# A hybrid attention trunk on one core: spare buffers for the last grouped head, work moved between VectorE and GpSimd, and a last tile in two parts

## The chip, the cores and the metric

One NeuronCore of a Trainium2 chip runs the whole program. The metric is device microseconds of one execution. A core has TensorE (PE in the profile, with its weight loads as PEld), VectorE (DVE), ScalarE (ACT), GpSimd (POOL) and SyncE (SP, which here issues nearly all DMAs). Each engine works through its own queue in order; semaphores order the queues among each other.

## The reference, cut to what matters

Two layers of a trunk with two token mixers side by side. There are 512 latent tokens and 256 context tokens, 1024 channels, and heads of 64. All data are float32.

```
hx = rmsnorm(x) * (1 + scale) + shift;  p = hx @ w_in        # all projections in one
a_att = neighbourhood attention of 8 heads (latent queries: window and all context keys)
b_att = grouped-query attention of 8 query heads over 2 key heads (all 768 keys)
o_a = (a_att * silu(a_z)) @ w_o_a ;  o_b = (b_att * silu(b_z)) @ w_o_b
merged = sigmoid(g_a) * o_a + sigmoid(g_b) * o_b
x = x + gate * (merged @ w_out)
```

Layer 0 does the same for the context tokens (they attend to the context alone); layer 1 needs only the latent ones, and what it gives is the output.

## The kernel before, in words

**High and low parts.** A float32 product is made of three TensorE products: each operand is split into a high part (a cast on ScalarE to a shorter float32) and a low part (the difference, on VectorE or GpSimd), and `mm3` (lines 351 to 353) adds high x high, high x low and low x high. A matrix of weights goes through a `raw` tile (three buffers, loaded by SP), then `whi` and `wlo` (a ring of eight each, in the pool `wp`). `load_w` and `load_w2` do this; their last argument picks the engine of the low part: `mix_lo` alternates GpSimd and VectorE, `pool_lo` takes GpSimd.

**Order.** The kernel is written in Python, and a planner turns it into the five queues: an instruction that stands earlier in the text has priority, later ones go ahead where the planner's model of time finds an engine free. Buffers come from rings: a tag has so many buffers, they are given out in the order of the text, and a tile waits until one is free.

**The stage around the change.** `pipeline` runs 8 grouped heads: `gq_scores(h)`, then `gq_values(h - 1)`, then a share of `fill` (pieces of the gates' and `w_o_a`'s projections, one bank `psf`). Behind the last scores come the rest of `fill`, then `early` (it splits quarters 0 to 2 of `zb` into `gbh` and `gbl` with `hilo`: cast on ScalarE, line 557; low part on GpSimd, line 558), and last `values_of(7)`.

`gq_values` handles six blocks of 128 keys. For each, `transpose_split` transposes the probabilities of the four query tiles with four TensorE products into a bank `pst` (line 669; two banks, tag `t`), ScalarE casts them to `pth` (line 672), VectorE forms `ptl` (line 673), both from rings of two, and TensorE adds two products into the bank `psv` (lines 972 and 973; one bank). In layer 0 a seventh block, `ctx_values`, follows for the context queries. `head_out` then copies one half of `psv` to `ho` (one buffer; line 681, ScalarE), adds the other half (line 682, VectorE) and multiplies the sum into `zb`, which holds the gate (line 683, GpSimd).

**The merge.** The banks of scores (`pss`, two of two banks each) and `psv` close, and five banks `psx` open. The last quarter of `zb` is split, and `o_chunks("b", ...)` multiplies it by `w_o_b`: four chunks of two `w_o_b` tiles, each chunk two column groups of four steps. `evac_b` merges into `tg` and splits the result into `mh` and `ml`. Then for each half `n` of `w_out` (eight tiles of 512 columns) and each tile `t` of 128 tokens, `tok_proj` runs 24 products, and `evac_o` multiplies by the gate (line 1039), adds `x` (line 1041) and, in layer 1, stores (line 1043).

Of the kernel before, what the change touches and what calls it, by code (L numbers as in the profile page):

```python
# [8 lines left out]
F32 = mybir.dt.float32  # L9
F32R = mybir.dt.float32r  # L10
BF16 = mybir.dt.bfloat16
AF = mybir.ActivationFunctionType
ALU = mybir.AluOpType
# [9 lines left out]
KT = DM // 128  # L23
# [35 lines left out]
def R(ap):  # L59
    return ap.bitcast(F32R)  # L60
# [7 lines left out]
def hybrid_kernel(es: ExitStack, tc, x, ctx, cvec, w_ada, w_ada0, small, gvec, w_in, w_o_a, w_o_b, w_out,  # L68
# [13 lines left out]
    def nm(s):  # L82
        uid[0] += 1
        return f"{s}_{uid[0]}"
# [26 lines left out]
    def psw(n=512, kind="w"):  # L111
        if kind == "w":
            kind = "f" if pm["i"] % pm["n"] == 0 else "x"
            pm["i"] += 1
        pool, cols = pm[kind]
        return pool.tile([128, cols], F32, tag=kind, name=nm("ps" + kind))[:, :n]
# [211 lines left out]
    def load_w2(src, col0, nk, lo_eng):  # L328

        res = []  # L330
        for i in range(nk // 2):
            raw = raw_tile()
            nc.sync.dma_start(raw.rearrange("p (k n) -> p k n", k=2),
                              src[256 * i:256 * i + 256, col0:col0 + 256].rearrange("(k p) n -> p k n", k=2))
            hi = wp.tile([128, 512], F32R, tag="whi", name=nm("whi"), bufs=8)
            S.copy(hi, raw)  # L336
            lo = wp.tile([128, 512], F32R, tag="wlo", name=nm("wlo"), bufs=8)
            lo_eng(i).tensor_tensor(lo, raw, F(hi), ALU.subtract)  # L338
            res += [(hi[:, c:c + 256], lo[:, c:c + 256]) for c in (0, 256)]
        return res  # L340
# [149 lines left out]
    def layer(l, hx, nxt, mid):  # L490
# [60 lines left out]
        def hilo_tiles(name):  # L551
            return [big(name + part).rearrange("p (f n) -> p f n", f=4) for part in "hl"]

        def hilo(src, dst, fs):
            sv = src.rearrange("p (f n) -> p f n", f=4)
            for f in fs:
                S.copy(R(dst[0][:, f, :ntok]), sv[:, f, :ntok])
                G.tensor_tensor(R(dst[1][:, f, :ntok]), sv[:, f, :ntok], dst[0][:, f, :ntok], ALU.subtract)

        def load_tg(c):  # L560
            nc.sync.dma_start(tg[c].rearrange("p (f n) -> p f n", f=4)[:, :, :ntok], gs[c][:, :, :ntok])
# [1 line left out]
        def o_chunks(br, prepare, evac):  # L563

            src = (w_o_a if br == "a" else w_o_b)[l]
            act = lambda part, k: gated[br][part][:, k, :]
            res = []
            for i in range(4):
                st = {}

                def ld(i=i, st=st):
                    st["w"] = load_w2(src, 256 * i, 4, mix_lo)
                pieces = [lambda f=f, n0=n0, n1=n1, i=i, st=st:
                          chan_proj(st["w"], f, act, n0, n1, lambda f, a, b, ps: evac(2 * i + f, a, b, ps))
                          for f in range(2) for n0, n1 in spans]
                res.append((ld, ([prepare] if i == 0 and prepare else []) + pieces))
            return res
# [72 lines left out]
        if True:  # L650
# [10 lines left out]

            def transpose_split(blocks, n0=0, n1=512):

                pt = psw(512, "t")
                for src, c0 in blocks:
                    if c0 is None:
                        T.transpose(pt.rearrange("p (s n) -> p s n", n=64)[:, 0:8:7, :], src, ident)
                    else:
                        T.transpose(pt[:, c0:c0 + 128], src, ident)  # L669
                hi = att["p"].tile([128, 512], F32R, tag="pth", name=nm("pth"), bufs=att["nt"])  # L670
                lo = att["p"].tile([128, 512], F32R, tag="ptl", name=nm("ptl"), bufs=att["nt"])
                S.copy(hi[:, n0:n1], pt[:, n0:n1])  # L672
                V.tensor_tensor(lo[:, n0:n1], pt[:, n0:n1], F(hi[:, n0:n1]), ALU.subtract)  # L673
                return hi, lo

            def head_out(po, e, dst):

                n = dst.shape[-1]
                m, o = 64 * e, 64 * (1 - e)
                t1 = att["p"].tile([128, 512], F32, tag="ho", name=nm("ho"), bufs=1)  # L680
                S.copy(t1[m:m + 64, :n], po[o:o + 64, :n])
                V.tensor_tensor(t1[m:m + 64, :n], po[m:m + 64, :n], t1[m:m + 64, :n], ALU.add)
                G.tensor_tensor(dst, dst, t1[m:m + 64, :n], ALU.mult)

            def rows(a, half):
                return a[64 * half:64 * half + 64]
# [69 lines left out]
            def open_att(name, width, n_p, n_t):  # L756
                st = ExitStack()
                att["p"] = st.enter_context(tc.tile_pool(name=name, bufs=2, reuse_waits="tile"))
                att["w"], att["np"], att["nt"] = width, n_p, n_t
                return st  # L760


# [74 lines left out]
            def pipeline(fill, spread, scores_of, values_of, last=None, bg=[]):  # L837

                n = len(fill)
                prev = None  # L840
                for h in range(8):
                    att["bg"] = bg if h > 3 or pm["n"] == 1 else []
                    st = scores_of(h)
                    if prev is not None:
                        values_of(h - 1, prev)
                    run(fill, len(fill) - (n - n * min(h + 1, spread) // spread))
                    prev = st
                if last is not None:
                    run(fill, len(fill))
                    last()  # L850
                run(bg, len(bg))
                values_of(7, prev)
                run(fill, len(fill))

# [140 lines left out]
        with tc.tile_pool(name=f"mrg{l}", bufs=1, reuse_waits="tile") as mp:  # L995
            open_ps(x=5)
            extra = lambda name: mp.tile([128, 3072], F32, tag="extra", name=nm(name))
            gv = mp.tile([128, nv, DM], F32, tag="gate", name=nm("gate"), bufs=1)
            for v in range(nv):
                src = gd[l][8 * v:8 * v + 8].rearrange("k p -> (k p)").unsqueeze(0)  # L1000
                nc.sync.dma_start(gv[:, v, :], src.to_broadcast([128, DM]))
            hilo(zb, gated["b"], [3])
            mg = []

            def evac_b(f, n0, n1, ps):
                a, b = tg_part(0, f, n0, n1), tg_part(1, f, n0, n1)
                V.scalar_tensor_tensor(b, b, 1.0, ps, ALU.add, ALU.mult)
                V.tensor_tensor(a, a, b, ALU.add)
                hi, lo = [m[:, f % 4, n0:n1] for m in mg[f // 4]]
                S.copy(R(hi), a)  # L1010
                V.tensor_tensor(R(lo), a, hi, ALU.subtract)
            chunks = o_chunks("b", None, evac_b)
            chunks[0][0]()
            for i in range(4):
                if i < 3:
                    chunks[i + 1][0]()
                if i % 2 == 0:
                    mg.append(hilo_tiles("m"))
                for piece in chunks[i][1]:
                    piece()  # L1020

            nt = 6 if first else 4
            xv = [a.rearrange("p (t n) -> p t n", t=3) for a in (big("xt0"), extra("xt1"))]
            xts = []
            for t in range(nt):
                xt = xv[t // 3][:, t % 3, :]
                nc.sync.dma_start(xt, x_src(t) if first else xs1[128 * t:128 * t + 128, :])
                xts.append(xt)
            a_m = lambda part, k: mg[k // 4][part][:, k % 4, :]
            bg = ada_steps(1, range(16), (1,), 2, mp) + [lambda: ada_mod(1)] if first else []  # L1030
            run(bg, 1)
            per_bg = -(-len(bg) // nt)
            for n in range(2):
                w = load_w(w_out[l], 512 * n, 512, KT, mix_lo)

                def evac_o(t, ps, n=n):
                    cs = slice(512 * n, 512 * n + 512)
                    t1 = mp.tile([128, 512], F32, tag="t1", name=nm("t1"), bufs=2)
                    V.tensor_tensor(t1, ps, gv[:, 0 if t < 4 else 1, cs], ALU.mult)
                    xt = xts[t]  # L1040
                    V.tensor_tensor(xt[:, cs], xt[:, cs], t1, ALU.add)
                    if not first:
                        nc.sync.dma_start(o_lat[16 * t:16 * t + 16][:, :, cs], xt[:, cs])
                    elif n == 1:
                        if t < 4:
                            nc.sync.dma_start(xs1[128 * t:128 * t + 128, :], xt)
                        late.append(lambda: make_hx(1, t, xt, nxt(), mp))
                late = []
                for t in range(nt):
                    tok_proj(w, 512, a_m, t, evac_o)  # L1050
                    run(bg, per_bg)
                    run(late, len(late) - 1)
                run(late, len(late))
# [186 lines left out]
```

## Time and profile before

| what | value |
|---|---|
| median of 3 runs | 1148.6 us (1148.3 to 1148.79) |
| the profiled execution, in full | 1149.07 us |
| its span in the profile | 1147.0 us |
| TensorE busy | 1123.5 us, 98% of the span |
| VectorE, ScalarE, GpSimd busy | 818.3, 580.3, 483.0 us |
| granted TensorE clock, mean | 0.999 |

A row of the timeline reads: start in us from the span's start, duration in us, engine, line, operation, what is written `<-` what is read, shapes, count, and in brackets the idle time of the engine ahead of it and who ended it. A row of the table of stretches reads: window, length, busy time of PE, PEld, DVE, ACT, POOL with instruction counts, granted clock, share of DMA time, GB/s. Rows of equal instructions close together are merged (x3), and their duration is then that of the group.

### The profile page before, as it was taken

What the parts mean: (1) busy time and instruction counts of PE and PEld (TensorE: products, weight loads), DVE (VectorE), ACT (ScalarE), POOL (GpSimd) and SP (SyncE); (2) the same over time, 40 slices, a digit from 0 to 9 for tenths busy, and PEclk for the clock granted to TensorE, in tenths of its full rate; (3) what the DMA queues carried; (4) which work ended last, traced back from release to release, by engine and by line L of the source; (5) the groups of instructions that cost most, each with busy time, mean ns of one, the idle gap of its engine ahead of it and who ended that gap; (6) DMA issues with size and microseconds to landing.
All of it is one profiled execution on the core that took longest, in us unless ns stands there. A gap on an engine that the chain in (4) does not pass through costs nothing.

```text
span 1147.0 us, 17434 instructions
## 1 busy us (share of the span) xinstructions
PE 1123.5 (98%) x6136; PEld 949.2 (83%) x6136; DVE 818.3 (71%) x1533; ACT 580.3 (51%) x1185; POOL 483.0 (42%) x449
## 2 busy tenths in 40 slices
PE   7999999999999999999999999999999999999998
PEld 5788888888988888888788787888888888887786
DVE  6777688997454786697588755469787665898563
ACT  6553366655433565665330355336666355766421
POOL 1073355453374343453411227345554664465311
PEclk9999999999999999999999999999999999999999
DMA  9645311333322232451434424633332333152143
GB/s 370 232 127 156 90 51 60 105 110 111 106 101 89 95 103 92 92 221 38 149 127 130 151 70 122 193 89 115 97 113 74 111 102 101 65 176 90 61 133 92
DMA packets 89695, 135.08 MB, mean 118 GB/s; under 512 B 10789, under 2 KB 52745, under 8 KB 88969
## 3 DMA queue, kind: packets, MB, share of 16 engines
q1 hardware_dynamic: 89328, 133.87, 36.8%
q8 instruction: 48, 0.79, 0.3%
q14 instruction: 39, 0.31, 0.1%
q10 hardware_dynamic: 280, 0.12, 0.0%
HBM read 116.63 MB, written 17.32 MB: 117 GB/s over the span
## 4 chain that ended last, share of the span: by engine, by line
PE 80%; DVE 7%; DMA 4%; issue 3%; ACT 3%; POOL 2%; SPq 0%; POOLq 0%; ACTq 0%; DVEq 0%
PE psx L353 12%; PE psx L352 12%; PE psx L351 11%; PE psf L351 9%; PE psf L352 9%; PE psf L353 9%; PE pst L669 4%; DMA raw<-in_w_in_dram 2%; PE pss L718 2%; PE pss L719 2%; PE psv L973 2%; PE psv L972 1%; PE pss L795 1%; PE pst L431 1%; DMA rawb<-in_w_ada_dram 1%
## 5 line engine op out<-in xcount | busy, mean ns | idle before, releaser
L673 DVE TENSOR_TENSOR ptl<-pst,pth 128x512 fp32r<-128x512 f32 (+1 forms) x176 | 115.9, 671 | 46.4 <-ACT pth L672 45.4
L672 ACT CAST pth<-pst 128x512 fp32r<-128x512 f32 (+1 forms) x176 | 99.3, 577 | 86.7 <-PE pst L669 55.8
L338 POOL TENSOR_TENSOR wlo<-raw,whi 128x512 fp32r<-128x512 f32 x68 | 95.6, 1409 | 105.1 <-ACT whi L336 83.9
L351 PE MATMUL psf<-hx,whi 128*128 128x512 f32 (+1 forms) x368 | 139.2, 378 | 0.6 <-ACT zt L516 0.6
L352 PE MATMUL psf<-hx,whi 128*128 128x512 f32 (+1 forms) x368 | 138.2, 375 | 0.0
L353 PE MATMUL psf<-hx,wlo 128*128 128x512 f32 (+1 forms) x368 | 137.8, 374 | 0.0
L351 PE MATMUL psx<-whi,hx 128*128 128x512 f32 (+1 forms) x368 | 137.6, 375 | 0.0
L353 PE MATMUL psx<-whi,hx 128*128 128x512 f32 (+1 forms) x368 | 135.9, 369 | 0.1
L352 PE MATMUL psx<-wlo,hx 128*128 128x512 f32 (+1 forms) x368 | 135.7, 369 | 0.0
L336 ACT CAST whi<-raw 128x512 fp32r<-128x512 f32 x136 | 82.7, 621 | 51.6 <-DMA raw<-in_w_in_dram 35.6
L321 ACT CAST whi<-raw 128x512 fp32r<-128x512 f32 x88 | 53.9, 623 | 99.6 <-PE psx L353 38.1
L669 PE MATMUL pst<-ident,p 128*128 128x128 f32 x640 | 99.9, 272 | 1.4 <-DVE ptl L673 0.8
L324 POOL TENSOR_TENSOR wlo<-raw,whi 128x512 fp32r<-128x512 f32 x36 | 50.9, 1416 | 110.0 <-ACT whi L321 74.6
L338 DVE TENSOR_TENSOR wlo<-raw,whi 128x512 fp32r<-128x512 f32 x68 | 68.6, 1010 | 28.1 <-ACT whi L336 27.2
L669 PEld LDWEIGHTS pst<-ident,p 128*128 128x128 f32 x640 | 77.8, 140 | 13.0 <-DVE ptl L673 1.3
L658 POOL TENSOR_SCALAR r<-r 128x1 f32<-128x1 f32 x64 | 22.4, 350 | 152.2 <-DVE r L653 145.2
L659 POOL TENSOR_TENSOR p<-p,r 128x512 f32<-128x512 f32 (+1 forms) x64 | 84.2, 1316 | 5.1
L353 PEld LDWEIGHTS psx<-whi,hx 128*128 128x128 f32 x368 | 69.4, 189 | 12.6 <-DVE hx L1137 1.0
L351 PEld LDWEIGHTS psx<-whi,hx 128*128 128x128 f32 x368 | 69.5, 189 | 12.4 <-issue 0.8
L353 PEld LDWEIGHTS psf<-hx,wlo 128*128 128x128 f32 x368 | 69.4, 188 | 11.8
L351 PEld LDWEIGHTS psf<-hx,whi 128*128 128x128 f32 x368 | 69.4, 189 | 11.4 <-ACT zt L516 0.8
L352 PEld LDWEIGHTS psx<-wlo,hx 128*128 128x128 f32 x368 | 69.5, 189 | 10.8
(252 smaller groups left out, 3056.0 us busy)
## 6 DMA issues: line engine op xcount, KB each, us to landing
raw<-in_w_in_dram SPq DMA_DIRECT2D x168, 256.0 KB, 2.9
rawb<-in_w_ada_dram SPq DMA_DIRECT2D x64, 256.0 KB, 2.9
gs<-zt SPq DMA_DIRECT2D x32, 256.0 KB, 2.1
raw<-in_w_out_dram SPq DMA_DIRECT2D x32, 256.0 KB, 2.9
tg<-gs SPq DMA_DIRECT2D x4, 1536.0 KB, 6.8
rawx<-in_w_ada_dram SPq DMA_DIRECT2D x8, 512.0 KB, 7.9
raw<-in_w_o_a_dram SPq DMA_DIRECT2D x16, 256.0 KB, 2.8
raw<-in_w_o_b_dram SPq DMA_DIRECT2D x16, 256.0 KB, 2.8
```

The lines of the kernel that those rows point to most:

```text
L321: S.copy(hi[:, :n], raw[:, :n])
L324: e.tensor_tensor(lo[:, :n], raw[:, :n], F(hi[:, :n]), ALU.subtract)
L336: S.copy(hi, raw)
L338: lo_eng(i).tensor_tensor(lo, raw, F(hi), ALU.subtract)
L351: T.matmul(ps, lhs[0], rhs[0], start=first, stop=False)
L352: T.matmul(ps, lhs[0], rhs[1], start=False, stop=False)
L353: T.matmul(ps, lhs[1], rhs[0], start=False, stop=last)
L659: G.tensor_tensor(p[:, c0:c1], p[:, c0:c1], r[:, i:i + 1].to_broadcast([128, c1 - c0]), ALU.mult)
L669: T.transpose(pt[:, c0:c0 + 128], src, ident)
L672: S.copy(hi[:, n0:n1], pt[:, n0:n1])
L673: V.tensor_tensor(lo[:, n0:n1], pt[:, n0:n1], F(hi[:, n0:n1]), ALU.subtract)
L718: T.matmul(ps[:, c0:c0 + n], q, sl(kh), start=True, stop=False)
```

## The change

It has five parts.

1. In `values_of(7)` of the grouped heads of both layers (`att["end"]`), every second transposed block is spare: its bank is one of the score banks, and its high and low parts are tiles of the weights' rings `whi` and `wlo`. A count over all blocks (`att["turn"]`) says which are spare.
2. In the same head the product with the gate moves from GpSimd to VectorE.
3. The split of the last quarter of `zb` takes its low part on VectorE.
4. The first chunk of `w_o_b` takes both its low parts on GpSimd; before, the second was on VectorE.
5. In layer 1 the last token tile of the second half of `w_out` is computed, gated, added and stored in two parts of 256 columns.

```diff
-        def hilo(src, dst, fs):
+        def hilo(src, dst, fs, lo=G):
...
-                G.tensor_tensor(R(dst[1][:, f, :ntok]), sv[:, f, :ntok], dst[0][:, f, :ntok], ALU.subtract)
+                lo.tensor_tensor(R(dst[1][:, f, :ntok]), sv[:, f, :ntok], dst[0][:, f, :ntok], ALU.subtract)
...
-                    st["w"] = load_w2(src, 256 * i, 4, mix_lo)
+                    st["w"] = load_w2(src, 256 * i, 4, pool_lo if br == "b" and i == 0 else mix_lo)
...
-                pt = psw(512, "t")
+                spare = att["end"] and att["turn"] % 2 == 1
+                att["turn"] += 1
+                pt = psw(512, "s" if spare else "t")
...
-                hi = att["p"].tile([128, 512], F32R, tag="pth", name=nm("pth"), bufs=att["nt"])
-                lo = att["p"].tile([128, 512], F32R, tag="ptl", name=nm("ptl"), bufs=att["nt"])
+                pool, th, tl, n = (wp, "whi", "wlo", 8) if spare else (att["p"], "pth", "ptl", att["nt"])
+                hi = pool.tile([128, 512], F32R, tag=th, name=nm(th), bufs=n)
+                lo = pool.tile([128, 512], F32R, tag=tl, name=nm(tl), bufs=n)
...
-                G.tensor_tensor(dst, dst, t1[m:m + 64, :n], ALU.mult)
+                (V if att["end"] else G).tensor_tensor(dst, dst, t1[m:m + 64, :n], ALU.mult)
...
+                att["end"], att["turn"] = False, 0
...
                 run(bg, len(bg))
+                att["end"] = last is not None
                 values_of(7, prev)
...
-            hilo(zb, gated["b"], [3])
+            hilo(zb, gated["b"], [3], V)
...
-                def evac_o(t, ps, n=n):
-                    cs = slice(512 * n, 512 * n + 512)
-                    t1 = mp.tile([128, 512], F32, tag="t1", name=nm("t1"), bufs=2)
+                def evac_o(t, ps, n=n, c=(0, 512)):
+                    cs = slice(512 * n + c[0], 512 * n + c[1])
+                    t1 = mp.tile([128, 512], F32, tag="t1", name=nm("t1"), bufs=2)[:, :c[1] - c[0]]
...
+                    if not first and n == 1 and t == nt - 1:
+                        for c in ((0, 256), (256, 512)):
+                            ps = psw(256)
+                            tok_mm(ps, [[a[:, c[0]:c[1]] for a in x] for x in w], 256, a_m, t, 0, KT)
+                            evac_o(t, ps, c=c)
+                        break
```

## The prediction

> **What bounds the kernel now.** I read the page first: its busy shares, then the clock row of its slices.
>
> ```profile
> span 1147.0 us, 17434 instructions
> PE 1123.5 (98%) x6136; PEld 949.2 (83%) x6136; DVE 818.3 (71%) x1533; ACT 580.3 (51%) x1185; POOL 483.0 (42%) x449
> PEclk9999999999999999999999999999999999999999
> ...
> L673 DVE TENSOR_TENSOR ptl<-pst,pth 128x512 fp32r<-128x512 f32 (+1 forms) x176 | 115.9, 671 | 46.4 <-ACT pth L672 45.4
> L672 ACT CAST pth<-pst 128x512 fp32r<-128x512 f32 (+1 forms) x176 | 99.3, 577 | 86.7 <-PE pst L669 55.8
> ```
>
> TensorE is busy 98% of the span at full granted clock. No edit here removes a matmul, so the change can win only where TensorE stands still. The two groups below are the cast and the low part of a transposed block, 577 and 671 ns each. Next I read the table of busy time by stretches, around both places where a grouped-head stage ends.
>
> ```profile
> 550.00:560.00 10.00, 9.22 (x57) 7.45 (x56) 6.76 (x9) 4.66 (x8) 7.13 (x5) 1.00 0.09 27
> 560.00:570.00 10.00, 8.80 (x50) 7.53 (x49) 3.17 (x7) 2.94 (x5) 5.12 (x4) 1.00 0.82 294
> ...
> 1040.00:1060.00 20.00, 18.46 (x100) 15.20 (x99) 17.79 (x26) 11.53 (x23) 11.01 (x10) 1.00 0.17 53
> 1060.00:1080.00 20.00, 18.77 (x98) 13.45 (x97) 11.81 (x18) 11.16 (x20) 6.20 (x7) 1.00 0.17 55
> ...
> 1120.00:1147.00 27.00, 21.56 (x96) 17.51 (x94) 9.37 (x13) 3.11 (x5) 2.59 (x2) 0.97 0.29 89
> ```
>
> The first number after the window is its length, the second TensorE's busy time. Three places lose time: the end of layer 0's grouped heads (550 to 570, 0.78 and 1.20, 1.98 us), the end of layer 1's (1040 to 1080, 2.77 us, more in truth, since a matmul's busy time includes its drain), and the tail after the last matmul. The timeline, cut to those places, says what each waits for.
>
> **The change part by part.** *Layer 0.*
>
> ```profile
> 552.79 5.87 POOL L558 TENSOR_TENSOR gbl<-zb,gbh 128x768 fp32r<-128x768 f32 x3 [3.60 <-PE psf L352]
> 553.40 1.78 DVE L338 TENSOR_TENSOR wlo<-raw,whi 128x512 fp32r<-128x512 f32 x1
> 554.40 0.48 PE L351 MATMUL psf<-gbh,whi 128*128 128x512 f32 x1
> ...
> 558.61 1.30 POOL L338 TENSOR_TENSOR wlo<-raw,whi 128x512 fp32r<-128x512 f32 x1
> 558.71 0.50 PE L352 MATMUL psf<-gbl,whi 128*128 128x512 f32 x1 [0.78 <-POOL gbl L558]
> 559.05 0.39 PE L353 MATMUL psf<-gbh,wlo 128*128 128x512 f32 x1
> ...
> 559.99 1.28 POOL L683 TENSOR_TENSOR zb<-zb,ho 64x512 f32<-64x512 f32 x1
> ...
> 561.30 0.36 ACT L681 COPY ho<-psv 64x256 f32<-64x256 f32 x1 [3.08 <-POOL zb L683]
> ...
> 562.18 0.50 PE L351 MATMUL psx<-gbh,whi 128*128 128x512 f32 x1 [1.20 <-DVE ho L682]
> ```
>
> The wait of 1.20 us is a chain: POOL forms the gate product of head 7 late (behind a weight's low part), the single ho buffer is then free for the context part, and only its sum frees the bank. With the product on VectorE right behind the head's own sum, ho is free before the context matmuls end. The product on VectorE shows in no row; the nearest are 0.67 (the low part of a block, also 512 columns) and 1.78 (the split at 553.40, beside POOL), against 1.28 on POOL. I take 0.67, as head 6's and 7's sums end clear of POOL's long run, and count the 1.20 as gone; at 1.78 it stays. The last low part of gb moves from POOL to VectorE too; it is wanted only after the pieces' first three quarters, so it counts nothing.
>
> The ring is the larger matter. Tiles of one tag are handed out in program order. The spare blocks of head 7 take places in the weights' ring ahead of all eight w_o_b tiles, so none of those can be split before the last spare block's cast. (Layer 0 has seven transposed blocks per head, so the count reaches head 7 odd, and blocks 0, 2, 4 and the context block are spare; layer 1 has six, and blocks 1, 3, 5 are.) Two things follow. The nine matmuls on gb between 554.40 and 559.05, which fill gaps of head 7 now, move behind it. And VectorE's 1.78 us split at 553.40, and POOL's at 558.61, leave this stretch and come after, POOL taking both halves of the first pair (that is the edit of the loader). The 0.78 wait for gbl goes, since its reader comes later; late next are the weights. POOL has its three gbl until 558.66, then two low parts of 1.30, until 561.3. TensorE meanwhile has the products that need only high parts: two weights' rows, two column groups, both spans, two of three products, which is 2 x 2 x 2 x (0.23 + 0.12) = 2.8 us. If head 7 ends near 557.4 (559.75 less nine matmuls of 0.23, plus some drain that nothing fills now, an estimate), that work lasts to 560.2 and the first low part is there at 559.96. I take 0.5 us of new wait and 0.5 of drain: layer 0 gives 1.20 + 0.78 - 1.0 = 1.0 us. Ends: a gain of 1.98, or a loss of 2.7 (1.98 won, 2.07 of filler moved to where nothing needs it, and both low parts, 2.6, waited for).
>
> *Layer 1.*
>
> ```profile
> 1017.25 0.62 ACT L336 CAST whi<-raw 128x512 fp32r<-128x512 f32 x1
> ...
> 1055.49 0.63 ACT L336 CAST whi<-raw 128x512 fp32r<-128x512 f32 x1
> ...
> 1045.06 0.68 DVE L338 TENSOR_TENSOR wlo<-raw,whi 128x512 fp32r<-128x512 f32 x1
> ...
> 1056.29 1.75 DVE L338 TENSOR_TENSOR wlo<-raw,whi 128x512 fp32r<-128x512 f32 x1
> 1056.42 0.48 PE L351 MATMUL psf<-gbh,whi 128*128 128x512 f32 x1
> ...
> 1058.69 0.50 PE L973 MATMUL psv<-ptl,vb 128*128 128x512 f32 x1 [1.54 <-DVE ptl L673]
> ...
> 1069.04 0.39 PE L353 MATMUL psf<-gbh,wlo 128*128 128x512 f32 x1
> 1069.73 0.60 PE L669 MATMUL pst<-ident,p 128*128 128x128 f32 x4
> ...
> 1073.44 0.60 PE L669 MATMUL pst<-ident,p 128*128 128x128 f32 x4
> 1074.65 0.60 PE L669 MATMUL pst<-ident,p 128*128 128x128 f32 x4
> 1075.78 0.60 PE L669 MATMUL pst<-ident,p 128*128 128x128 f32 x4
> ...
> 1078.12 0.40 PE L351 MATMUL psx<-gbh,whi 128*128 128x512 f32 x1
> ```
>
> The eight w_o_b casts lie between 1017.25 and 1055.49; all move behind block 5 of head 7. With the last goes the 1.75 us split that stands ahead of ptl at 1056.29: the 1.54 us wait is gone. Head 7 runs from 1069.73 to 1078.12, 8.4 us. Its transposes come 1.21 and 1.13 us apart, while four transposes (0.44) and two products (0.46) are 0.90 us of TensorE; the rest is the wait for one of two banks through cast and low part. With every second block elsewhere, four blocks can be under way. Then VectorE limits: six low parts and head 6's sum at 0.67 are 4.7 us, plus 1.3 to the first (four transposes, 0.66, and a cast, 0.58) and 0.5 for the last product, 6.5 us. Gain 1.9 (ends 0 and 2.4, the latter at 1.0 us a block). Against it, nine filler matmuls between 1056.42 and 1069.04 move behind: 9 x 0.23 = 2.07, and I count all of it, since the heads before run at the two-bank pace with or without it. Weights: block 5's cast ends 1.1 us before the head's end (1.24 after its transposes start, at 1075.78 now, of 2.34 to 1078.12); the first pair then takes two casts of 0.62 and two low parts of 1.30 on a POOL that is free. The first low part is there 0.8 us after the head's end, and 8 high-part products of 0.23, 1.84 us, cover that. Layer 1 gives 1.54 + 1.9 - 2.07 = 1.4 us; ends a gain of 2.6 (if a third of the filler was in the way) and a loss of 1.8 (no faster head, 1.3 waited for).
>
> Later loads: b0 and b1's first tile sit in the three raw buffers; the others follow as POOL frees them, and w_out behind. On SP's queue the w_out loads move from before the head to after it. Two tiles serve 24 matmuls, 5.5 us, against a load, cast and low part of some 5 us for three buffers, so I count nothing.
>
> *Rule and row.* A 512-column low part on VectorE took 0.68 us at 1045.06 and 1.75 beside POOL's work at 1056.29, while ptl, which reads a bank, shows no such case. The Trainium skill, "SBUF — State Buffer", section "SBUF: two separate sides", says that a VectorE step with two SBUF inputs and a GpSimd step exclude each other for the whole instruction; the rows agree, and by it the moved gate product could wait out a low part on POOL. That rule gives the third rival below.
>
> *Tail.*
>
> ```profile
> 1136.64 0.39 PE L351 MATMUL psx<-whi,mh 128*128 128x512 f32 x1
> ...
> 1141.17 0.39 PE L353 MATMUL psx<-whi,ml 128*128 128x512 f32 x1
> 1141.60 0.69 DVE L1039 TENSOR_TENSOR t<-psx,gate 128x512 f32<-128x512 f32 x1 [3.80 <-PE psx L353]
> 1142.32 0.69 DVE L1041 TENSOR_TENSOR xt<-xt,t 128x512 f32<-128x512 f32 x1
> ...
> 564.35 0.28 PE L351 MATMUL psx<-gbh,whi 128*128 128x256 f32 x1
> 565.42 0.40 PE L351 MATMUL psx<-gbh,whi 128*128 128x512 f32 x1
> 569.72 0.42 DVE L1008 TENSOR_TENSOR tg<-tg,tg 128x256 f32<-128x256 f32 x1
> ```
>
> The view of the DMAs has each issue's size and the median time from issue to landing:
>
> ```profile
> gs<-zt SPq DMA_DIRECT2D x32, 256.0 KB, 2.1
> gs<-zt SPq DMA_DIRECT2D x16, 128.0 KB, 2.9
> ```
>
> Twenty 512-wide steps take 4.53 us, 0.227 each; nine 256-wide ones 1.07, 0.119 each. So 24 become 48 and 5.44 us become 5.71: a loss of 0.27. The last two VectorE steps shrink from 1.38 to 0.84: a gain of 0.54. The store of half the columns has 1 KB runs; the two rows of gs say that it could land 0.8 us later, or no later. I take 0. Tail: a gain of 0.3, ends 0.6 and -0.5.
>
> **Sum.** 1.0 + 1.4 + 0.3 = 2.7 us. The profiled execution took 1149.07 us (1147.0 of span, 2.1 around it), 0.5 over the median of 1148.6: 1146.4 on its own scale, 1145.9 on the median's. About 0.2%, 2.3 us, is what a measurement of this kernel can tell from no change.
>
> **Rivals.** *Late weights* (slower). For it: all w_o_b splits stand behind the head, and POOL has 5.87 us of gbl in front of them in layer 0. It decides from the point where the second low part ends after the 2.8 us of high-part products do and the planner does not reorder around it. Layer 0 loses 2.7, layer 1 1.8, the tail gives 0.3: 1152.8. Against it: in layer 1 POOL is free. *No faster head* (no change): if cast and low part, not banks, set the pace, layer 1 gives 1.54 - 2.07 = -0.5, layer 0 1.0, the tail 0.3: 1147.8. For it: ACT and VectorE need 0.58 and 0.67 per block, one after the other; against: the longer is well under 1.17. *The product waits for POOL*: the gate product of layer 0 starts only when a step of POOL ends, up to 1.3 later, so the 1.20 stays: 1147.1. *All covered*: 1.98 + 2.6 + 0.6, 1143.4.
>
> **How the numbers follow.** Forecast 0.48, late weights 0.14, no faster head 0.18, product waits 0.10, all covered 0.10. The forecast's own range is 1144.5 to 1147. It lies only 0.4 us beyond the bound, so 0.04 of its chance goes to no change: faster 0.10 + 0.44, no change 0.18 + 0.10 + 0.04, slower 0.14. The range 1143.6 to 1149.8 leaves out some of both ends.
>
> **What would show it.** In the timeline of after: the w_o_b casts behind head 7's blocks; no wait for DVE ho near 562 nor for ptl near 1058; transposes of head 7 about 0.9 us apart; psf on gbh only after psv; at the end two 256-wide sums and a store of 128 KB. A wait of TensorE for wlo or whi at the start of the w_o_b pieces makes the forecast wrong, as does an order of the planner that differs elsewhere.

## The result and the profile after

| kernel | median | ratio to before (95%) |
|---|---|---|
| before | 1148.58 us (20 runs) | |
| changed | 1147.28 us (20 runs) | 0.9985 [0.9979, 0.9992] |

The change wins 1.3 us by the medians, 0.15% by the ratio. The interval lies clear of 1, but the gain is less than the 0.2% that the prediction counts as a difference; it is inside its range, and half of the 2.7 us forecast. The small number hides larger ones of both signs. The page of the changed kernel first (the last two lines are the low part and the cast of a transposed block; its line numbers are 2 to 5 higher than before from line 669 on):

```profile
span 1145.5 us, 17478 instructions
...
PE 1121.8 (98%) x6160; PEld 950.3 (83%) x6160; DVE 819.6 (72%) x1538; ACT 579.7 (51%) x1185; POOL 479.7 (42%) x446
...
PEclk9999999999999999999999999999999999999999
...
L676 DVE TENSOR_TENSOR ptl<-pst,pth 128x512 fp32r<-128x512 f32 (+1 forms) x169 | 111.3, 671 | 45.2 <-ACT pth L675 44.1
...
L675 ACT CAST pth<-pst 128x512 fp32r<-128x512 f32 (+1 forms) x169 | 95.1, 577 | 85.6 <-PE pst L671 57.7
```

Seven blocks (four of layer 0, three of layer 1) have left the `ptl` group, 176 to 169; the duration of one is the same. The table of stretches of the changed kernel, for the windows shown of before:

```profile
550.00:560.00 10.00, 7.96 (x41) 6.04 (x40) 5.92 (x7) 4.79 (x8) 7.66 (x6) 1.00 0.32 105
560.00:570.00 10.00, 8.54 (x48) 7.28 (x47) 6.36 (x9) 1.86 (x4) 4.81 (x3) 1.00 0.55 199
1040.00:1060.00 20.00, 19.93 (x111) 16.38 (x110) 15.12 (x25) 10.79 (x22) 7.19 (x7) 1.00 0.00 0
1060.00:1080.00 20.00, 17.47 (x93) 13.29 (x92) 13.60 (x21) 13.62 (x26) 11.95 (x10) 1.00 0.29 95
```

Layer 0's two windows got worse (TensorE 9.22 and 8.80 us busy before, 7.96 and 8.54 now), layer 1's first got better (18.46 to 19.93) and its second worse (18.77 to 17.47). Windows at fixed times mix in work that moved from one to the next, so the price of each part is read from the stages further down. Why layer 0 lost stands in its timeline, cut to what matters:

```profile
553.40 0.39 PE L978 MATMUL psv<-wlo,vb 128*128 128x512 f32 x1
553.62 0.28 PE L351 MATMUL psf<-gah,whi 128*128 128x256 f32 x1
...
554.93 0.28 PE L353 MATMUL psf<-gah,wlo 128*128 128x256 f32 x1
...
552.44 1.29 POOL L338 TENSOR_TENSOR wlo<-raw,whi 128x512 fp32r<-128x512 f32 x1 [1.78 <-PE psv L978]
554.30 1.29 POOL L338 TENSOR_TENSOR wlo<-raw,whi 128x512 fp32r<-128x512 f32 x1 [0.56 <-ACT whi L336]
555.54 6.30 POOL L558 TENSOR_TENSOR gbl<-zb,gbh 128x768 fp32r<-128x768 f32 x3
...
557.13 0.39 PE L749 MATMUL psv<-whi,vb 128*128 128x256 f32 x1 [0.91 <-DVE ho L685]
557.95 2.20 DVE L686 TENSOR_TENSOR zb<-zb,ho 64x512 f32<-64x512 f32 x1
559.65 0.50 PE L352 MATMUL psf<-gbl,whi 128*128 128x512 f32 x1 [1.08 <-POOL gbl L558]
560.18 2.21 DVE L338 TENSOR_TENSOR wlo<-raw,whi 128x512 fp32r<-128x512 f32 x1
560.24 0.36 ACT L684 COPY ho<-psv 64x256 f32<-64x256 f32 x1 [1.03 <-DVE zb L686]
562.42 0.43 DVE L685 TENSOR_TENSOR ho<-psv,ho 64x256 f32<-64x256 f32 x1
562.90 0.50 PE L351 MATMUL psx<-gbh,whi 128*128 128x512 f32 x1 [1.46 <-DVE ho L685]
```

Head 7's spare blocks (`psv<-whi`, `psv<-wlo`) now run ahead of the last pieces on `gah`. The last of those starts at 554.93 instead of 552.54, two low parts for `w_o_b` get onto GpSimd first, and its run of three `gbl` starts at 555.54 instead of 552.79 and ends at 561.84. The gate product on VectorE falls into that run and takes 2.20 us. TensorE has three waits there, 0.91, 1.08 and 1.46 us, where before there were two, 0.78 and 1.20. The longest ends with the context queries' sum (562.42): ScalarE's copy for it was done at 560.60, but VectorE was at a low part of `w_o_b`, which had fallen into GpSimd's run too (560.18, 2.21 us).

To put every kernel on one scale I cut its one profiled execution at six points: A, from head 5's second sum (`ho`, 534.50 before) to the last product on `gb` of layer 0; B, from there to layer 1's first product on `hx`; C, to its last; D, to layer 1's last product on `gb`; E, to the last product of all; F, to the end of the span. Stages in us:

| kernel (run) | A: layer 0's heads, w_o_b | B: w_out of layer 0 | C | D: layer 1's heads, w_o_b | E | F | median |
|---|---|---|---|---|---|---|---|
| before | 58.00 | 68.65 | 343.92 | 92.58 | 43.52 | 5.86 | 1148.58 |
| changed | 59.69 | 69.14 | 343.33 | 90.56 | 43.96 | 4.61 | 1147.28 |
| tail_only | 58.03 | 69.03 | 343.03 | 92.59 | 43.96 | 4.61 | 1147.89 |
| ns_loader_mixed | 57.26 | 69.04 | 343.09 | 92.61 | 43.96 | 4.59 | 1146.91 |
| ns_pool_product | 58.03 | 69.23 | 343.25 | 91.59 | 43.96 | 4.60 | 1146.81 |
| ns_last_low_pool | 57.27 | 70.19 | 343.58 | 91.63 | 43.96 | 4.59 | 1148.07 |
| no_spare | 57.24 | 68.87 | 343.27 | 91.59 | 43.96 | 4.59 | 1146.01 |
| bank_only | 57.09 | 69.06 | 343.30 | 90.94 | 43.96 | 4.59 | 1145.39 |
| gbl_vector | 59.20 | 68.62 | 343.27 | 90.51 | 43.96 | 4.60 | 1146.90 |
| l0_pool_product | 60.26 | 68.79 | 343.22 | 90.60 | 43.96 | 4.60 | 1148.64 |
| l1_only | 58.01 | 69.41 | 343.22 | 90.55 | 43.95 | 4.61 | 1145.98 |
| l0ns_gbl_vector | 57.37 | 69.70 | 343.15 | 90.49 | 43.96 | 4.59 | 1145.52 |
| l0_no_spare | 57.24 | 68.68 | 343.07 | 90.52 | 43.96 | 4.59 | 1144.71 |
| bank0_ring1 | 57.08 | 68.60 | 343.21 | 90.51 | 43.96 | 4.59 | 1144.47 |

Stage A repeats to 0.03 us and stage D to 0.11 wherever the edits in them are the same (58.00, 58.03, 58.01; 90.49 to 90.60), so differences of 0.1 us in A and of 0.2 in D can be read. That is finer than the medians, whose intervals often overlap from one run to the next. Stage B wanders between 68.60 and 70.19, even between kernels with the same order of TensorE (l0_no_spare and l0ns_gbl_vector, 68.68 and 69.70). C and the time ahead of A, which no edit touches, add up to between 877.40 and 878.42. Between before and changed, A costs 1.69, D wins 2.02 and the tail (E and F) 0.81: a gain of 1.14 us. B costs 0.49, and C and the time ahead of A win 0.88, both no more than they wander. Together 1.5, the difference of the spans.

### The profile page after: what moved, and what is told of

Its sections match the earlier page's. It is cut to its first block, busy times and chain, and to the rows that moved or that the text cites. A ratio compares the mean times of both kernels' runs of the same rounds, so it can differ in the third digit from the quotient of the medians.

```text
span 1145.5 us, 17478 instructions
## 1 busy us (share of the span) xinstructions
PE 1121.8 (98%) x6160; PEld 950.3 (83%) x6160; DVE 819.6 (72%) x1538; ACT 579.7 (51%) x1185; POOL 479.7 (42%) x446
## 4 chain that ended last, share of the span: by engine, by line
PE 84%; DVE 5%; DMA 4%; issue 3%; POOL 2%; ACT 2%; SPq 0%; POOLq 0%; ACTq 0%; DVEq 0%
PE psx L351 12%; PE psx L353 12%; PE psx L352 12%; PE psf L351 10%; PE psf L352 9%; PE psf L353 9%; PE pst L671 5%; PE pss L721 2%; PE pss L722 2%; PE psv L978 2%; PE psv L977 2%; PE pss L799 1%; PE pst L431 1%; DMA raw<-in_w_in_dram 1%; DMA rawb<-in_w_ada_dram 1%
## 5 line engine op out<-in xcount | busy, mean ns | idle before, releaser
L676 DVE TENSOR_TENSOR ptl<-pst,pth 128x512 fp32r<-128x512 f32 (+1 forms) x169 | 111.3, 671 | 45.2 <-ACT pth L675 44.1
L338 POOL TENSOR_TENSOR wlo<-raw,whi 128x512 fp32r<-128x512 f32 x70 | 98.2, 1407 | 102.3 <-ACT whi L336 76.6
L675 ACT CAST pth<-pst 128x512 fp32r<-128x512 f32 (+1 forms) x169 | 95.1, 577 | 85.6 <-PE pst L671 57.7
L324 POOL TENSOR_TENSOR wlo<-raw,whi 128x512 fp32r<-128x512 f32 x36 | 50.6, 1406 | 118.5 <-ACT whi L321 73.2
L671 PE MATMUL pst<-ident,p 128*128 128x128 f32 x612 | 95.5, 272 | 1.5 <-DVE ptl L676 1.0
L338 DVE TENSOR_TENSOR wlo<-raw,whi 128x512 fp32r<-128x512 f32 x66 | 64.3, 976 | 29.4 <-ACT whi L336 29.0
L671 PEld LDWEIGHTS pst<-ident,p 128*128 128x128 f32 x612 | 74.3, 141 | 12.0 <-DVE ptl L676 1.2
```

The source lines that it names most:

```text
L324: e.tensor_tensor(lo[:, :n], raw[:, :n], F(hi[:, :n]), ALU.subtract)
```

## The experiments

The first four ask which layer and which edit loses. The theory: layer 0 loses 2 us because spare blocks delay the gate pieces and with them GpSimd's `gbl`; layer 1 and the tail win. Rivals: the product on VectorE is layer 0's loss; or the tail is the whole gain.

**l1_only.** Edits 1 to 4 in layer 1 alone.

```diff
-                att["end"] = last is not None
+                att["end"] = last is not None and not first
-                    st["w"] = load_w2(src, 256 * i, 4, pool_lo if br == "b" and i == 0 else mix_lo)
+                    st["w"] = load_w2(src, 256 * i, 4, pool_lo if br == "b" and i == 0 and not first else mix_lo)
-            hilo(zb, gated["b"], [3], V)
+            hilo(zb, gated["b"], [3], G if first else V)
```

> The edits of the grouped heads (spare blocks, VectorE's gate product and last low part, POOL's loader) act in layer 1 alone; the tail's two parts stay. Theory T: the two traces put a loss of about 2.1 us on layer 0, a gain of about 2.0 on the end of layer 1's heads and 0.8 on the tail. With layer 0 as before, layer 0's end returns to about 661.2 us in the trace and the time is 1147.3 - 2.1 = 1145.2 us. Rival R3 (the tail alone gains, the heads' edits cancel by chance in both layers): between 1147 and 1148.

Measured: 1145.98 us, 0.9977 [0.9967, 0.9986]. Stages A (58.01) and D (90.55) are as the theory says. The time is 0.8 above its 1145.2, and stage B came out 0.8 above before's. The tail is not the whole gain.

**l0_pool_product.** The changed kernel with layer 0's gate product on GpSimd.

```diff
-                (V if att["end"] else G).tensor_tensor(dst, dst, t1[m:m + 64, :n], ALU.mult)
+                (V if att["end"] and not first else G).tensor_tensor(dst, dst, t1[m:m + 64, :n], ALU.mult)
```

> The changed kernel, but head 7's gate product of layer 0 goes back to GpSimd. Rival R1 (the VectorE product of 2.20 us beside GpSimd is what layer 0 loses): the wait of 1.46 us for ho at 562.90 goes and the time falls by about 1.4, to 1145.9. Theory T (the three gbl low parts of 6.3 us on GpSimd start 2.75 us later because head 7's spare blocks run ahead of the last gate pieces): the product queues behind those low parts on GpSimd, ends no sooner, and the time stays or rises, 1147.3 to 1148.6.

Measured: 1148.64 us, 0.9999 [0.999, 1.0008]; the product on VectorE is not the loss. The trace (GpSimd, then TensorE) shows the queue that the theory names: the product stands behind the three `gbl` and starts at 562.79.

```profile
556.44 6.27 POOL L558 TENSOR_TENSOR gbl<-zb,gbh 128x768 fp32r<-128x768 f32 x3
562.79 1.29 POOL L686 TENSOR_TENSOR zb<-zb,ho 64x512 f32<-64x512 f32 x1
564.99 0.50 PE L351 MATMUL psx<-gbh,whi 128*128 128x512 f32 x1 [0.44 <-DVE ho L685]
```

**l0_no_spare.** The changed kernel with spare blocks in layer 1 only.

```diff
-                spare = att["end"] and att["turn"] % 2 == 1
+                spare = att["end"] and not first and att["turn"] % 2 == 1
```

> The changed kernel, but without spare blocks in layer 0: there all of head 7's blocks take the two old banks again, while the gate product on VectorE, the last low part and GpSimd's loader stay. Theory T: the order of the last gate pieces and of gbl returns to that of before, the three gbl start near 552.8 us and layer 0 comes back by most of its 2.1 us: 1145.2 (1144.7 to 1146). Rival R1 (the product on VectorE is the loss): the time stays at about 1147.3.

Measured: 1144.71 us, 0.9965 [0.9953, 0.9978]. The spare blocks are layer 0's loss, and more: without them stage A is 0.76 shorter than before (57.24). Its rows:

```profile
553.17 5.87 POOL L558 TENSOR_TENSOR gbl<-zb,gbh 128x768 fp32r<-128x768 f32 x3 [3.60 <-PE psf L352]
559.10 0.50 PE L352 MATMUL psf<-gbl,whi 128*128 128x512 f32 x1 [0.79 <-POOL gbl L558]
559.48 1.36 DVE L686 TENSOR_TENSOR zb<-zb,ho 64x512 f32<-64x512 f32 x1
561.81 0.50 PE L351 MATMUL psx<-gbh,whi 128*128 128x512 f32 x1 [0.42 <-DVE ho L685]
```

`gbl` starts right behind the gate pieces again, the product starts behind its run, beside GpSimd's next step, and takes 1.36 us, and the wait for `ho` falls from 1.20 to 0.42.

**tail_only.** The kernel before with the last token tile in two parts.

```diff
+                    if not first and n == 1 and t == nt - 1:
+                        for c in ((0, 256), (256, 512)):
...
+                        break
```

> The kernel before with the last token tile in two parts and nothing else. Theory T: a gain of 0.8 us by the two traces (last gb matmul to the end of the span 49.35 before, 48.57 after), 1147.8. Rival R3 (the heads' edits cancel, the tail is the whole gain): 1147.3. The prediction's step said 0.3, 1148.3.

Measured: 1147.89 us, 0.9994 [0.9985, 1.0003]; against 1148.76 of the runs beside it 0.87, though the interval reaches past 1. The stages say it sharper: F falls from 5.86 to 4.61, E rises from 43.52 to 43.96.

The next four ask what about the spare blocks costs layer 0, and what else wins in layer 1.

**gbl_vector** and **l0ns_gbl_vector.** Layer 0's third `gbl` low part on VectorE, in the changed kernel and in l0_no_spare.

```diff
-                hilo(zb, gated["b"], range(3))
+                [hilo(zb, gated["b"], [f], V if first and f == 2 else G) for f in range(3)]
```

> The changed kernel, with the third of layer 0's three gbl low parts on VectorE; GpSimd keeps two. Theory T (in layer 0 the spare blocks make GpSimd's three gbl start at 555.5 and run to 561.8, and that run is what TensorE then waits for): the run ends some 2 us earlier, the wait of 1.08 us for gbl goes and the gate product is no longer beside it at its end, a gain of 1 to 2 us, 1145.3 to 1146.3. Rival (the loss is the order of head 7 and the filler, not GpSimd): within 0.4 us of 1147.3.

> Spare blocks in layer 1 alone, and the third gbl low part of layer 0 on VectorE; TensorE's order stays the same as without that move. If the wait of 0.79 us for gbl at 559.10 is the end of GpSimd's run of three (theory T): it goes, 1144.0. Rival (VectorE's step beside GpSimd takes about 2 us, as the split at 553.78 did with 1.78, and delays ptl or ho of head 7): 1144.7 to 1146.

Measured: 1146.90 us, 0.9985 [0.9976, 0.9993], and 1145.52 us, 0.9972 [0.9961, 0.9983]. My strong form of the theory (GpSimd's run is what TensorE waits for) falls: stage A gives back 0.49 us in the one, of the 2.45 that leaving out the spare blocks gives back (59.69 to 57.24), and loses 0.13 in the other. Both came out as their rivals said. Rows of gbl_vector:

```profile
555.08 1.26 DVE L558 TENSOR_TENSOR gbl<-zb,gbh 128x768 fp32r<-128x768 f32 x1 [0.84 <-PE psf L352]
555.49 4.77 POOL L558 TENSOR_TENSOR gbl<-zb,gbh 128x768 fp32r<-128x768 f32 x2
556.73 0.51 PE L351 MATMUL psf<-gbh,whi 128*128 128x512 f32 x1 [1.10 <-DVE tg L592]
560.31 0.50 PE L352 MATMUL psf<-gbl,whi 128*128 128x512 f32 x1 [1.27 <-POOL gbl L558]
```

Two steps on GpSimd beside VectorE take 4.77 us (three took 5.87 in l0_no_spare), and VectorE is late for `tg`, which holds the bank `psf`: a new wait of 1.10. In l0ns_gbl_vector, where TensorE's order is unchanged, the 0.79 for `gbl` goes and waits of 0.32 and 0.73 for `gbl` and `ho` come.

**bank_only.** The changed kernel with the spare blocks in a score bank, but in `pth` and `ptl` as before and not in the weights' ring.

```diff
-                pool, th, tl, n = (wp, "whi", "wlo", 8) if spare else (att["p"], "pth", "ptl", att["nt"])
+                pool, th, tl, n = att["p"], "pth", "ptl", att["nt"]
```

> The changed kernel, but the spare blocks of both layers only go to a score bank; their two halves stay in pth and ptl and not in the weights' ring. Theory T (the ring places, ahead of the w_o_b tiles, make head 7's blocks due early and so push the last gate pieces of w_o_a back): layer 0's order returns to that of before and layer 0 comes back by about 2 us, while layer 1 gets its w_o_b splits back into the stretch before head 7 and loses up to 1.5 us: 1145.3 to 1147. Rival (the bank by itself does it): layer 0 as in the changed kernel, 1147.3 or more.

Measured: 1145.39 us, 0.9972 [0.9961, 0.9984]. The halves in the weights' ring are the loss: stage A goes from 59.69 to 57.09. Beside the product on VectorE the bank takes away what is left of layer 0's two waits (0.79 and 0.42 in l0_no_spare) for waits of 0.18 at 556.63 and 0.50 at 559.18; the stage is 0.15 shorter for it. In its timeline the gate pieces stand ahead of the head's blocks again:

```profile
553.34 0.28 PE L353 MATMUL psf<-gah,wlo 128*128 128x256 f32 x1
553.46 0.40 PE L977 MATMUL psv<-pth,vb 128*128 128x512 f32 x1
...
553.58 5.87 POOL L558 TENSOR_TENSOR gbl<-zb,gbh 128x768 fp32r<-128x768 f32 x3 [3.15 <-PE psf L352]
559.18 0.38 PE L749 MATMUL psv<-pth,vb 128*128 128x256 f32 x1 [0.50 <-DVE ho L685]
```

**no_spare.** The changed kernel without spare blocks: `spare = False`.

> The changed kernel without spare blocks in either layer; the product on VectorE, the last low part on VectorE, GpSimd's loader and the tail's two parts stay. Beside the kernel with spare blocks in layer 1 alone (1144.7) it prices them there. Theory T (spare blocks are the gain of layer 1's end): 1146.8 (1146.2 to 1147.2), which is the gain of layer 0's product 0.9 and of the tail 0.9. Rival (product, last low part and loader make layer 1's gain): 1144.7 to 1145.3.

Measured: 1146.01 us, 0.9977 [0.9968, 0.9985], between the two. Spare blocks are worth 1.07 us in stage D (91.59 to 90.52), and another edit is worth 1.0.

The last four name it, and put the best parts together. Three undo one edit each in no_spare.

**ns_loader_mixed.** `pool_lo if br == "b" and i == 0 else mix_lo` becomes `mix_lo`.

> No spare blocks in either layer and the loader of the first pair of w_o_b as before (its second low part on VectorE); product, last low part and tail stay. TensorE's order is the same as with GpSimd's loader. Theory L: the loader is what gains 0.99 us from layer 1's head stage beside the tail alone (the split of 1.76 us on VectorE at 1021.16 goes to GpSimd and the loss of 0.9 us of TensorE near 1028 to 1039 with it): 1146.0 + 0.9 = 1146.9. Rival (the product or the last low part on VectorE): 1146.0.

Measured: 1146.91 us, 0.998 [0.9971, 0.9989]: theory L. Stage D is 92.61 again. What moved is one split, long before the last head; first ns_loader_mixed (VectorE, then TensorE), then no_spare (GpSimd), whose TensorE has no wait in that stretch:

```profile
1019.92 1.77 DVE L338 TENSOR_TENSOR wlo<-raw,whi 128x512 fp32r<-128x512 f32 x1
...
1027.00 0.50 PE L351 MATMUL psf<-gah,whi 128*128 128x512 f32 x1 [0.28 <-DVE tg L592]
```

```profile
1021.43 1.28 POOL L338 TENSOR_TENSOR wlo<-raw,whi 128x512 fp32r<-128x512 f32 x1
```

The order of TensorE is the same in both. Only 0.28 of the 1.02 us shows as a wait; the rest lies in later starts that no wait marks (0.55 us behind no_spare just after this wait, 1.00 by 1038.4). In the changed kernel no split of `w_o_b` stands in that stretch: its first cast there starts at 1066.19, behind the spare blocks. By that order the ring would have taken the split away from VectorE there with the old loader too, and no run has spare blocks with the old loader. So the loader's 1.02 us holds for kernels whose splits stay where they were; how loader and ring share the gain in the changed kernel stays open.

**ns_pool_product.** The gate product on GpSimd (`G.tensor_tensor`).

> No spare blocks, head 7's gate product back on GpSimd in both layers; last low part, loader and tail stay. Theory: the product on VectorE is what shortens layer 0's stage by 0.76 us (the wait for ho there is 1.20 with GpSimd's product and 0.42 with VectorE's): 1146.0 + 0.8 = 1146.8. Rival (the last low part on VectorE or the loader does it): 1146.0.

Measured: 1146.81 us, 0.9984 [0.9975, 0.9993]. Stage A returns to 58.03, stage D stays: the product is worth 0.79 us in layer 0 and nothing in layer 1.

**ns_last_low_pool.** `hilo(zb, gated["b"], [3])`, its low part on GpSimd.

> No spare blocks, the last low part of gb back on GpSimd in both layers; product, loader and tail stay. The prediction counts this edit at nothing: 1146.0. Rival (GpSimd's 1.3 us or more for it is waited for by the last quarter of the w_o_b products): 1146.4 to 1147.

Measured: 1148.07 us, 0.9995 [0.9986, 1.0003]. Its own stages don't move (57.27 and 91.63), so nothing there waits for it; but the order of TensorE behind it differs from no_spare's, and in stage B (70.19) TensorE has a wait that no other run has, for the next layer's normed tile:

```profile
646.86 1.09 PE L303 MATMUL pst<-ident,y 128*128 128x128 f32 x8 [1.51 <-DVE y L297]
```

Stage B is 1.3 us longer than no_spare's, of the 2.06 between the medians. Since that stage wanders by 1.0 us without any change of order, the new order is a likely cause and not a shown one; the profiled execution took 1147.41, and the rest stays open.

**bank0_ring1.** In layer 0 the bank alone, in layer 1 bank and ring.

```diff
-                pool, th, tl, n = (wp, "whi", "wlo", 8) if spare else (att["p"], "pth", "ptl", att["nt"])
+                pool, th, tl, n = (wp, "whi", "wlo", 8) if spare and not first else (att["p"], "pth", "ptl", att["nt"])
```

> The changed kernel, but layer 0's spare blocks keep their two halves in pth and ptl and use the score bank only; layer 1's use bank and weights' ring. From the stages of two earlier runs: layer 0's heads as with banks only (57.09 us from head 6's sum to the last product on gb, against 57.24 without spare blocks), layer 1's as with ring (90.5): 1144.7 - 0.15 = 1144.5, the fastest of all. If bank and ring are not the cause, and the runs without them differ by the planner's luck: 1145 to 1147.

(Stage A starts at head 5's second sum; the expectation says head 6's.) Measured: 1144.47 us, 0.9961 [0.9948, 0.9973], an interval clear of the changed kernel's: this version beats both.

## Why the prediction was partly right

The sign was right and the time lies in the range, but the gain is half of the forecast, and its parts are not the forecast's. The forecast was +1.0 from layer 0, +1.4 from layer 1, +0.3 from the tail; the stages gave -1.69, +2.02 and +0.81. That the total still came out near is in part luck: an error of 2.7 us in layer 0 met errors of 0.6 and 0.5 the other way. Another 0.49 stands in stage B, where the first load of `w_out` starts at 557.95 instead of 540.61; the stage wanders by more, so no cause is shown. Of the prediction's signs, the end of the wait for `ptl` and the tail in two parts came; the casts behind all of head 7, the end of the wait for `ho` near 562 and `psf` on `gbh` only after `psv` did not, and the planner's order did differ elsewhere.

**Layer 0, the failed step.** The prediction said "Tiles of one tag are handed out in program order", and that no `w_o_b` tile can be split before the last spare block's cast. That held. The step that failed is what it drew from it: the splits "leave this stretch and come after", with head 7's blocks where they were. What moved is the blocks. Rows of the changed kernel:

```profile
539.19 1.26 ACT L675 CAST whi<-pss 128x512 fp32r<-128x512 f32 x2 [0.90 <-PE pss L671]
540.34 1.14 ACT L336 CAST whi<-raw 128x512 fp32r<-128x512 f32 x2
```

The last spare cast is the second of the first row; head 7's last cast started at 557.03 before. The eight casts of `w_o_b` follow right behind, from 540.34 to 558.59 (502.44 to 552.74 before), and so their low parts crowd into the end of head 7: on GpSimd ahead of `gbl` (552.44 and 554.30), on VectorE within `gbl`'s run (557.13 and 560.18). That, and the blocks ahead of the gate pieces, pushed the run 2.75 us back, onto the product. With it fell the sentence "I take 0.67, as head 6's and 7's sums end clear of POOL's long run", which took that run to stay at 552.79. Head 7 did end near 557.4 as forecast (last `psv` 557.60), but because its blocks had moved ahead of the gate pieces: the number is luck.

bank_only against changed prices the halves in the ring at 2.60 us of stage A, and these two runs differ in nothing else. In the ring the halves have a place in its order and also tiles beyond the two of `pth` and `ptl`; no run has spare tiles outside the ring, so which of the two lets the planner pull the blocks ahead is argued, not shown. Undisturbed, the step on the product was of the right kind: the product on VectorE wins 0.79 where 1.20 was forecast, and takes 1.36 there, not 0.67.

**The product's price.** It took 0.69 us in layer 1 (at 1079.28, with GpSimd idle), 1.36 in l0_no_spare, 2.20 in the changed kernel. The GpSimd step that it met, taken singly, first in l0_no_spare, then in the changed kernel (the second of the three `gbl`):

```profile
559.00 1.29 POOL L338 TENSOR_TENSOR wlo<-raw,whi 128x512 fp32r<-128x512 f32 x1
```

```profile
557.32 2.28 POOL L558 TENSOR_TENSOR gbl<-zb,gbh 128x768 fp32r<-128x768 f32 x1
```

These steps end at 560.29 and 559.60, the product at 560.84 and 560.15: 0.55 us behind in both, though it had started 0.48 us into the one and 0.63 into the other. That is the pattern of a wait for the running step, and not of a slower rate. The Trainium skill, "SBUF — State Buffer", section "SBUF: two separate sides", says that of a VectorE step with two SBUF inputs and a GpSimd step that reads SBUF the one that comes second is blocked for the whole instruction of the other; the trace agrees, with the 0.55. This was the third rival: its time, 1147.1, is what came out, but by another sum, since it left layer 0 at a loss of 0.2 and layer 0 lost 1.69.

**Layer 1.** The wait of 1.54 for `ptl` at 1058.69 is gone, as forecast, and the spare blocks are the reason: no_spare still has it (1.54), bank_only has 0.71 of it. That nine filler products "move behind" head 7 did not happen: as in layer 0, the spare blocks were transposed early, from 1056.79 on, `w_o_b`'s casts follow right behind the last spare cast, and the filler stands ahead of the head's own products. Rows of the changed kernel:

```profile
1056.79 0.27 PE L671 MATMUL pss<-ident,p 128*128 128x128 f32 x1
...
1065.72 0.59 ACT L675 CAST whi<-pss 128x512 fp32r<-128x512 f32 x1
1066.19 1.67 ACT L336 CAST whi<-raw 128x512 fp32r<-128x512 f32 x3
...
1067.39 0.48 PE L351 MATMUL psf<-gbh,whi 128*128 128x512 f32 x1
...
1072.88 0.66 PE L671 MATMUL pst<-ident,p 128*128 128x128 f32 x4 [0.95 <-DVE ptl L676]
1073.47 0.50 PE L977 MATMUL psv<-pth,vb 128*128 128x512 f32 x1
1076.13 0.39 PE L978 MATMUL psv<-wlo,vb 128*128 128x512 f32 x1
...
1079.30 0.50 PE L351 MATMUL psx<-gbh,whi 128*128 128x512 f32 x1 [0.70 <-DVE ho L685]
```

The last head's twelve products stand in one burst, with starts from 1073.47 to 1076.13 and no wait for a bank. In place of the 1.54 stand 0.95 for `ptl` and 0.70 for `ho`. The 2.07 of filler was booked as work moved behind the head, and it wasn't moved there; the three terms of the spare blocks (1.54 and 1.9, less 2.07) come to 1.37 in the prediction and to 1.07 as measured (0.65 for the bank, 0.42 for the ring). The other half of stage D's gain came with an edit that the prediction costed only as a delay. Without spare blocks that is the loader, 1.02 us, by taking 1.77 us off VectorE near 1020, some 50 us ahead of the last head; with them the ring takes the same split away, as said above.

**Tail.** Right in sign, 0.81 instead of 0.3. The end of the changed kernel:

```profile
1140.89 0.28 PE L353 MATMUL psx<-whi,ml 128*128 128x256 f32 x1
1141.20 0.42 DVE L1044 TENSOR_TENSOR t<-psx,gate 128x256 f32<-128x256 f32 x1 [1.87 <-PE psx L353]
1141.66 0.42 DVE L1046 TENSOR_TENSOR xt<-xt,t 128x256 f32<-128x256 f32 x1
```

E costs 0.44 (0.27 forecast). F wins 1.25: about 0.53 from the two VectorE steps, where 0.54 was forecast; 0.12 from the shorter drain (last product to first step 0.43 before, 0.31 now); and 0.60 behind the last step (1143.01 to 1147.03 before, 1142.08 to 1145.50 now), where the prediction took the store at nothing. The list of DMA issues of tail_only has that term:

```profile
out_dram<-xt SPq DMA_DIRECT2D x7, 256.0 KB, 2.8
out_dram<-xt SPq DMA_DIRECT2D x2, 128.0 KB, 2.3
```

Half the bytes land 0.5 us sooner; the prediction's `gs` rows (2.9 for 128 KB against 2.1 for 256) were the wrong neighbours. The Trainium skill, "SBUF — State Buffer", section "The DMA setup-cost knee", gives a fixed 2 us plus bytes over 436 GB/s; an estimate from it is 2.3 and 2.6 us, and the trace agrees within 0.2.

**The last low part** was costed at nothing, and its own stages agree; undone, the median is 2.06 us higher, with 1.3 of it in a stage whose order differs, which no row near the edit could show.

## What to carry to other kernels

A spare buffer borrowed from another ring also borrows that ring's place in the order, and the planner can meet that order by moving the borrower: in both layers the weights' casts stood right behind the last spare cast, because the blocks had moved ahead. Here the bank alone won in both layers (0.15 and 0.65 us), while the ring won 0.4 in layer 1 and lost 2.6 in layer 0, so price the two apart and layer by layer. When work moves between VectorE and GpSimd, look for the long runs of the other engine at the new place, after asking whether the same change moves those runs. And follow a step off a busy engine along the whole stretch where it ran, not only to the next wait: the loader's 1.0 us without spare blocks came from one split taken off VectorE some 50 us ahead of the head.

## What the runs showed of the hardware

A 64x512 product of two SBUF operands on VectorE took 0.69 us with GpSimd idle; where it met a running GpSimd step it ended 0.55 us after that step, and so took 1.36 or 2.20. The reverse shows too. A `gbl` step on GpSimd took 1.84 us where it ran alone or had started first (563.88 and 552.79 before), but 2.29 where a VectorE step of two SBUF operands was ahead of it, and it then ended 1.70 us after that step (556.88 after 555.18 before; 561.84 after 560.15 in the changed kernel). And stage B differed by 1.0 us between two executions with the same order of TensorE (l0_no_spare and l0ns_gbl_vector): a wait of 0.3 us there in the one, of 0.5 and 0.9 in the other, all for parts of `w_out`, whose casts start as their loads land. That the landing varies is the likely cause; it wasn't tested.
